# Two score levels and odd tokens' own scores in one matmul, even tokens' own scores by a sum over partitions

## The chip, the cores and the metric

The kernel runs on one core of one Trainium2 chip, as one launch. The metric is the device time of that core in microseconds (us). A core has TensorE for matmuls (PE in the profile, PEld for its weight loads), VectorE (DVE), ScalarE (ACT), GpSimd (POOL), and SyncE (SP), whose queue issues most of the transfers here. Each works through its own queue in order; semaphores tie the queues together. Matmul results land in PSUM, everything else lives in SBUF, both with 128 partitions.

## The reference

One step of a decoder layer: a gated feed-forward block, a mixer with two kinds of recurrences, and a second feed-forward block, for 256 tokens of a new sequence (the prompt) and 8 sequences of 4 new tokens each (the samples, 32 tokens). The change lies in the recurrences of the mixer:

```python
def gated_linear_scan(q, k, v, log_a, s0):
    """S_t = diag(exp(log_a_t)) S_{t-1} + k_t^T v_t ; o_t = q_t S_t."""
    ...
    def step(s, inp):
        qi, ki, vi, gi = inp
        cum = jnp.cumsum(gi, axis=2)
        diff = cum[:, :, :, None, :] - cum[:, :, None, :, :]
        decay = jnp.where(causal, jnp.exp(jnp.where(causal, diff, 0.0)), 0.0)
        scores = jnp.sum(qi[:, :, :, None, :] * ki[:, :, None, :, :] * decay, axis=-1)
        o = (jnp.einsum('bhts,bhsv->bhtv', scores, vi)
             + jnp.einsum('bhtd,bhdv->bhtv', qi * jnp.exp(cum), s))
```

The score of the tokens t and s (s not after t) is the sum over the 128 key dimensions d of q[t,d] k[s,d] times the product of the decay factors of the tokens s+1 to t. For s = t it is plainly q[t] k[t], the token's own score. There are 4 heads with 256 values (GLA) and 8 heads with 128 values (HGRN2).

## The kernel before, in words

All matrices with tokens are held transposed: feature on the partition, the 288 tokens (256 of the prompt, then 32 of the samples) along the row. A dense product is a loop over 16 tiles of the input (`block`, L455 on). Its weights come from HBM by SP's queue (L61, L63), are split into a high and a low part by ScalarE (L86, `wh`) and VectorE (L87, `wl`), and each product is three matmuls with 288 moving columns (L464 to L466). These are the large matmuls of this document. A block works on four PSUM tiles out of a pool of five (`mmp`), and its evacuation (`evac`) reads them at its end.

The mixer runs the blocks `qk0`, `v0`, `qk1`, `v1`, `hfq0`, `hi0`, `hfq1`, `hi1`, `hfq2`, `hfq3` and four `gate` blocks. The recurrences are six scans of two heads each (two for GLA, four for HGRN2). A scan is a Python generator. `block` calls `tick` after each of its 16 input tiles, that is after 12 large matmuls, and a tick runs the generator to its next `yield`, so that scan work is written between the large matmuls. A scheduler then sets the final order on each engine: it can move an instruction ahead of or behind others of its engine, as its data and buffers allow.

A scan finds the scores by doubling. At level `lv`, with h = 2^lv, the tokens lie in pairs of runs of h tokens: scores between a left run and the right run beside it are one level's share. `Q` is q times the decay since the start of its run, `k` is scaled by the decay to the end of its run; `update(lv)` (L803) multiplies the right halves of `Q` and the left halves of `k` by the factors that take them to the next level. Steps 0 to 8 of a scan:

- step 0: `own` (L790) multiplies k with q, 128 by 128 tokens, four matmuls (two heads, two halves of the prompt) into the PSUM tile `sc_d`; only the diagonal is wanted. VectorE forms Q = q * f (L873).
- step n, for n from 1 to 8: `score(n-1)` (L817) multiplies `k` (up to 128 weight columns) with the right-half columns of `Q` (64 moving columns), again four matmuls; at levels 0 and 1 also two small ones for the samples (L836), and at level 0 two for the samples' own scores (L840). Then the result of the step before goes to the score matrix `Dg` (prompt) and `Ds` (samples) by predicated copies under the masks `mk` (`own_put` L800, `put` L844: L855, L861, L865). Then `update(n-1)`: L811 for `Q`, L813 for `k`, L815 for the factors.

Level 7 is written to `X`, a part of the tile `rp` (L847). PSUM tiles of the scans come from a pool of three (`aux`), which transposes, output products and norms share. After step 8 come the transposes of the keys (`key_t`), the output products (`out`), the new states (`final`, `sample`) and the heads' norms (`norm_a` to `norm_c`). The samples' states are loaded by SP (L787) into four buffers `s0`, each of which comes free when POOL has stored the state before (L975); ScalarE and VectorE split a loaded state (L950, L951).

Two buffer names matter besides. `z` and `mx` are tags of a pool with two buffers each: `z` holds the scaled result of an `hfq` or `gate` evacuation, `mx` an intermediate of the `hfq` evacuation (L1125 to L1130) and of `norm_c` (L1014). The masks are loaded once as integers (`mi32`, L690) and cast to bytes by POOL (`mk`, L706).

Of the kernel before, what the change touches and what calls it, by code (L numbers as in the profile page):

```python
# [16 lines left out]
P = 128  # L17
# [98 lines left out]
def trunk_kernel(ctx, tc, x_prompt, x_sample, state_gla, state_hgrn, norm_gains, f1_in, f1_out, f2_in, f2_out,  # L116
# [540 lines left out]
    def mixer(pn, border):  # L657
        with ExitStack() as mx:
# [26 lines left out]
            def setup():  # L685
# [18 lines left out]
                G.memset(Dg, 0.0)  # L704
                G.memset(Ds, 0.0)
                G.tensor_copy(mk, mi32)  # L706
                for a in range(2):
# [56 lines left out]
            def scan(d, Vt, V32, Vs, gla, ytile0, s0, sp_out, ss_out):  # L764
# [24 lines left out]

                def own():  # L790
                    ps = auxtile("sc_d")
                    for i in range(2):
                        for a in range(2):
                            c = (i * 2 + a) * P
                            PE.matmul(ps[:, c:c + P], k[:, a, i * P:(i + 1) * P], q[:, a, i * P:(i + 1) * P],
                                      start=c == 0, stop=True, skip_group_check=True)
                    return ps

                def own_put(ps):
                    V.copy_predicated(Dflat, mk[:, 448:576].unsqueeze(1).broadcast_to([P, 4, P]),  # L800
                                      ps.rearrange("p (a c) -> p a c", c=P))

# [14 lines left out]
                def score(lv):  # L817
# [8 lines left out]
                    for i in range(2):  # L826
                        for a in range(2):
# [3 lines left out]
                                      start=c == 0, stop=True, skip_group_check=True)  # L831
                    if h <= 2:
                        for a in range(2):
                            c = 256 + a * 16
                            r = Q[:, a, TP:T].rearrange("p (n two k) -> p n two k", two=2, k=h)[:, :, 1, :]
                            PE.matmul(ps[0:TS, c:c + 16], k[:, a, TP:T], r, start=False, stop=True, skip_group_check=True)  # L836
                    if h == 1:
                        for a in range(2):
                            c = 288 + a * TS
                            PE.matmul(ps[0:TS, c:c + TS], k[:, a, TP:T], q[:, a, TP:T],  # L840
                                      start=False, stop=True, skip_group_check=True)
                    return ps

                def put(lv, ps):  # L844
# [4 lines left out]
                    if h == 64:  # L849
# [6 lines left out]
                                      ps[0:n, 0:256].rearrange("p (j n k) -> p j n k", j=4, k=h))  # L856
                    if h <= 2:
                        dst = Ds[0:TS].rearrange("p a (n two k) -> p (a n) two k", two=2, k=h)[:, :, 1, :]
                        n = 16 // h
                        for a in range(2):  # L860
                            V.copy_predicated(dst[:, a * n:(a + 1) * n, :],  # L861
                                              m[0:TS, 0:16].rearrange("p (n k) -> p n k", k=h),
                                              ps[0:TS, 256 + a * 16:272 + a * 16].rearrange("p (n k) -> p n k", k=h))
                    if h == 1:
                        V.copy_predicated(Ds[0:TS], mk[0:TS, 448:448 + TS].unsqueeze(1).broadcast_to([TS, 2, TS]),  # L865
                                          ps[0:TS, 288:352].rearrange("p (a c) -> p a c", c=TS))

                K3 = acc[:, 0:6 * TS].rearrange("p (a n t) -> p a n t", a=2, n=3)
                pss = {}
                for step in range(LEVELS + 1):  # L870
                    if step == 0:
                        pss[-1] = own()
                        V.tensor_tensor(Q, q, d["f"], op=ALU.mult)  # L873
                    else:
                        pss[step - 1] = score(step - 1)
                        if step == 1:
                            own_put(pss.pop(-1))
                        else:
                            put(step - 2, pss.pop(step - 2))
                        update(step - 1)  # L880
# [233 lines left out]
            def ev_hgrn(d, g):  # L1114
                def ev(f, ps):
                    z = tmp.tile([P, T], F32, name="z", tag="z")
                    ls = tmp.tile([P, T], F32, name="lsg", tag="lsg")
                    V.tensor_tensor(z, ps, rt, op=ALU.mult)
                    log_sigmoid(ls, z)
                    if f >= 2:  # L1120
                        act(ls, ls, AF.Exp)
                        V.scalar_tensor_tensor(d["q"][:, f - 2, :], z, QSCALE, ls, op0=ALU.mult, op1=ALU.mult)
# [4 lines left out]
                    V.tensor_tensor(m, ls, z, op=ALU.subtract)  # L1127
                    act(m, m, AF.Exp)
                    act(ls, ls, AF.Exp)
                    V.tensor_scalar(d["k"][:, f, :], m, omlb[:, hd:hd + 1], None, op0=ALU.mult)  # L1130
                    V.tensor_scalar(d["f"][:, f, :], ls, omlb[:, hd:hd + 1], lb[:, hd:hd + 1], op0=ALU.mult, op1=ALU.add)
# [144 lines left out]
```

## Time and profile before

| | |
|---|---|
| median of 3 runs | 2314.31 us (2312.02 to 2318.01) |
| profiled execution | 2314.71 us |
| its span | 2312.9 us |
| granted TensorE clock, mean | 0.997 |
| busy: TensorE, VectorE, ScalarE | 99%, 61%, 44% of the span |

The span is the time from the first to the last instruction of the profiled execution; its own time also counts what lies around them. Busy times count an engine while an instruction of it is in flight; matmuls overlap, so TensorE's cost of a matmul is read from the distance between starts and not from the duration shown. A line of a view names the engine, the line of the kernel, the operation and `out<-in` by the program's names. The chain of waits follows the work that ended last back to its releasers. The page itself and the other views are quoted in the prediction, where they are used.

### The profile page before, as it was taken

Reading aid. Unit: us, or ns where it says so; the run is one execution under the profiler, and the core shown is the slowest. Engines: PE = TensorE matmul, PEld = TensorE weight load, DVE = VectorE, ACT = ScalarE, POOL = GpSimd, SP = SyncE. Lnnn points to the kernel's source line nnn. Section 1 sums busy time; section 2 is a strip of 40 time slices with the busy share of each in tenths; the row PEclk is TensorE's granted clock in tenths of the full one; section 3 lists DMA queues with packets and bytes.
Section 4 is the critical chain, followed back from the end, with each engine's and each line's share of the span. In section 5 each row is a group of like instructions: output and inputs, shape, how many; then the busy total and the mean of one; then the engine's idle time right before and its main releaser. Section 6 shows DMA issues by size and latency. Waiting matters only on the chain.

```text
span 2312.9 us, 42140 instructions
## 1 busy us (share of the span) xinstructions
PE 2291.0 (99%) x17352; PEld 2276.1 (98%) x17352; DVE 1421.2 (61%) x2314; ACT 1012.7 (44%) x1555; POOL 64.4 (3%) x110
## 2 busy tenths in 40 slices
PE   9999999999999999999999999999999999999998
PEld 8999999999999999999999999999999999999998
DVE  7545545554556568787889854854555555545545
ACT  6443333333334446454555554544333333333345
POOL 0000000000000001001001100100000000000000
PEclk9999999999999999999999999999999999999999
DMA  7555555555555545555555555455555555555553
GB/s 214 164 166 164 165 166 168 168 165 164 167 167 186 157 151 159 152 152 171 149 169 156 159 184 167 129 160 172 165 165 167 169 164 163 165 164 166 165 164 115
DMA packets 217008, 378.16 MB, mean 163 GB/s; under 512 B 15362, under 2 KB 52400, under 8 KB 216816
## 3 DMA queue, kind: packets, MB, share of 16 engines
q1 hardware_dynamic: 211264, 365.48, 52.6%
q0 software_dynamic: 3376, 9.81, 1.3%
q8 instruction: 136, 2.23, 0.4%
q10 hardware_dynamic: 2176, 0.18, 0.1%
q14 instruction: 56, 0.46, 0.1%
HBM read 363.62 MB, written 11.80 MB: 162 GB/s over the span
## 4 chain that ended last, share of the span: by engine, by line
PE 94%; DVE 3%; issue 1%; DMA 1%; ACT 1%; POOL 0%; DVEq 0%; SPq 0%; POOLq 0%; ACTq 0%
PE gate L465 9%; PE gate L466 9%; PE gate L464 9%; PE out L465 8%; PE out L466 8%; PE out L464 8%; PE up L466 8%; PE up L464 8%; PE up L465 8%; PE hfq L464 2%; PE hfq L465 1%; PE mo L466 1%; PE mo L464 1%; PE mo L465 1%; PE hfq L466 1%; PE sc L830 1%
## 5 line engine op out<-in xcount | busy, mean ns | idle before, releaser
L87 DVE TENSOR_TENSOR wl<-raw,wh 128x1024 fp32r<-128x1024 f32 (+1 forms) x674 | 821.1, 1219 | 629.1 <-ACT wh L86 626.5
L86 ACT ACTIVATE wh<-raw 128x1024 fp32r<-128x1024 f32 (+1 forms) x674 | 711.3, 1056 | 1073.3 <-PE gate L465 323.9
L465 PE MATMUL gate<-xl,wh 128*128 128x288 f32 x1660 | 489.2, 295 | 0.2 <-DVE xl L243 0.2
L464 PE MATMUL gate<-xh,wh 128*128 128x288 f32 x1660 | 488.4, 296 | 0.7 <-DVE z L1174 0.5
L466 PE MATMUL gate<-xh,wl 128*128 128x288 f32 x1660 | 488.7, 295 | 0.2 <-DVE wl L87 0.2
L465 PE MATMUL out<-hl,wh 128*128 128x288 f32 x1408 | 415.8, 295 | 0.0
L464 PE MATMUL out<-hh,wh 128*128 128x288 f32 x1408 | 415.6, 295 | 0.0
L466 PE MATMUL up<-xh,wl 128*128 128x288 f32 x1408 | 415.0, 295 | 0.0
L466 PE MATMUL out<-hh,wl 128*128 128x288 f32 x1408 | 415.0, 295 | 0.0
L464 PE MATMUL up<-xh,wh 128*128 128x288 f32 x1408 | 414.6, 294 | 0.3 <-DVE g L523 0.3
L465 PE MATMUL up<-xl,wh 128*128 128x288 f32 x1408 | 414.8, 295 | 0.0
L465 PEld LDWEIGHTS gate<-xl,wh 128*128 128x128 f32 x1660 | 311.7, 188 | 1.1 <-DVE xl L243 1.0
L464 PEld LDWEIGHTS gate<-xh,wh 128*128 128x128 f32 x1660 | 310.5, 188 | 1.6 <-DVE z L1174 0.7
L466 PEld LDWEIGHTS gate<-xh,wl 128*128 128x128 f32 x1660 | 311.4, 188 | 0.7 <-DVE wl L87 0.7
L466 PEld LDWEIGHTS out<-hh,wl 128*128 128x128 f32 x1408 | 264.7, 188 | 0.0
L464 PEld LDWEIGHTS up<-xh,wh 128*128 128x128 f32 x1408 | 264.1, 188 | 0.6 <-DVE g L523 0.5
L464 PEld LDWEIGHTS out<-hh,wh 128*128 128x128 f32 x1408 | 264.6, 188 | 0.0
L465 PEld LDWEIGHTS out<-hl,wh 128*128 128x128 f32 x1408 | 264.5, 188 | 0.0
L466 PEld LDWEIGHTS up<-xh,wl 128*128 128x128 f32 x1408 | 264.2, 188 | 0.1
L465 PEld LDWEIGHTS up<-xl,wh 128*128 128x128 f32 x1408 | 264.2, 188 | 0.1
L583 DVE TENSOR_TENSOR y<-out,y 128x288 f32<-128x288 f32 x288 | 121.4, 452 | 104.5 <-PE out L466 101.7
L464 PE MATMUL hfq<-xh,wh 128*128 128x288 f32 x256 | 78.7, 307 | 0.0
(342 smaller groups left out, 2581.6 us busy)
## 6 DMA issues: line engine op xcount, KB each, us to landing
raw<-in_ffn_w_in_dram SPq DMA_DIRECT2D x352, 512.0 KB, 3.6
raw<-in_ffn_w_out_dram SPq DMA_DIRECT2D x176, 512.0 KB, 3.7
raw<-in_mix_w_in_dram SPq DMA_DIRECT2D x64, 512.0 KB, 3.7
raw<-in_mix_w_in_dram SPq DMA_DIRECT2D x96, 256.0 KB, 3.3
raw<-in_mix_w_out_dram SPq DMA_DIRECT2D x32, 512.0 KB, 3.8
out_dram<-s POOLq DMA_DIRECT2D x32, 256.0 KB, 3.3
s<-in_state_gla_dram SPq DMA_DIRECT2D x16, 256.0 KB, 3.6
s<-in_state_hgrn_dram SPq DMA_DIRECT2D x16, 256.0 KB, 3.4
```

Source lines behind the costliest of these rows:

```text
L86: i1 = self.nc.scalar.activation(h[:, c], raw[:, c], AF.Copy).ins
L87: i2 = self.nc.vector.tensor_tensor(l[:, c], raw[:, c], h[:, c].bitcast(F32), op=ALU.subtract).ins
L464: yield lambda: PE.matmul(dst, w[0][:, c:c + P], parts[0], start=start, stop=False)
L465: yield lambda: PE.matmul(dst, w[0][:, c:c + P], parts[1], start=False, stop=False)
L466: yield lambda: PE.matmul(dst, w[1][:, c:c + P], parts[0], start=False, stop=stop)
L583: V.tensor_tensor(y[k], ps, y[k], op=ALU.add)
L830: PE.matmul(ps[0:m, c:c + 64], k[:, a, i * P:i * P + m], r, start=c == 0, stop=True, skip_group_check=True)
```

## The change

Levels 0 and 1 and the own scores of odd tokens are computed by one group of four matmuls, and the own scores of even tokens by an elementwise product that a matmul with a matrix of equal entries sums over the partitions.

After `update(0)`, `k` of odd tokens is still the plain k, and `k` of even tokens carries the factor of the token behind it. So the product of this `k` with the plain q of odd tokens holds both: at s = t the own score of the odd token, at s = t - 1 its level-0 score. The same `k` with the right halves of `Q` after `update(0)` is level 1. A new tile `R` holds the two sets of 64 columns side by side, `R[:, a, 0]` the plain q of odd tokens and `R[:, a, 1]` the right halves of `Q` for level 1, copied by ScalarE (`lay`). The level-0 mask gets the diagonal of the odd tokens added. `rp` holds, before it is needed for `X`, the product of q and k of the even tokens, 144 columns for each head.

```diff
@@ setup @@
                 G.memset(Ds, 0.0)
+                V.tensor_tensor(mi32[:, 0:64], mi32[:, 0:64],
+                                mi32[:, 448:576].rearrange("p (n two) -> p n two", two=2)[:, :, 1], op=ALU.max)
                 G.tensor_copy(mk, mi32)
@@ scan @@
-                def own():
-                    ps = auxtile("sc_d")
+                R = sp[0].tile([P, 2, 2, T // 2], F32, name="R", tag="R", bufs=1)
+                own = rp.rearrange("p (a c) -> p a c", a=2)
+                def lay(lv, src):
+                    h = 1 << lv
+                    S.activation(R[:, :, lv, :].rearrange("p a (n k) -> p a n k", k=h), halves(src, h, True), AF.Copy)
+                def score01():
+                    ps, po = auxtile("sc01"), auxtile("sc_o")
                     for i in range(2):
                         for a in range(2):
                             c = (i * 2 + a) * P
-                            PE.matmul(ps[:, c:c + P], k[:, a, i * P:(i + 1) * P], q[:, a, i * P:(i + 1) * P],
+                            PE.matmul(ps[:, c:c + P], k[:, a, i * P:(i + 1) * P], R[:, a, :, i * 64:(i + 1) * 64],
                                       start=c == 0, stop=True, skip_group_check=True)
-                    return ps
-                def own_put(ps):
-                    V.copy_predicated(Dflat, mk[:, 448:576].unsqueeze(1).broadcast_to([P, 4, P]),
-                                      ps.rearrange("p (a c) -> p a c", c=P))
+                    PE.matmul(po[:, 0:T], onesD, rp, start=True, stop=True, skip_group_check=True)
+                    for a in range(2):
+                        c = T + a * TS
+                        PE.matmul(po[0:TS, c:c + TS], k[:, a, TP:T], R[:, a, :, P:P + TS // 2],
+                                  start=False, stop=True, skip_group_check=True)
+                    return ps, po
+                def put01(ps, po):
+                    ...
+                    for i in range(2):
+                        V.copy_predicated(v[:, i, :, :, 0], eye(P, 64).unsqueeze(1).broadcast_to([P, 2, 64]),
+                                          ov[:, :, i * 64:(i + 1) * 64])
+                    V.copy_predicated(sv[:, :, :, 0], eye(TS, 16).unsqueeze(1).broadcast_to([TS, 2, 16]),
+                                      ov[0:TS, :, P:])
+                    for lv in range(2):
+                        ...
+                        V.copy_predicated(dst, m.rearrange("p (n k) -> p n k", k=h).unsqueeze(1).broadcast_to(dst.shape),
+                                          ps.rearrange("p (j l n k) -> p j l n k", j=4, l=2, k=h)[:, :, lv])
+                        dst = Ds[0:TS].rearrange("p a (n two k) -> p a n two k", two=2, k=h)[:, :, :, 1, :]
+                        for a in range(2):
+                            c = T + a * TS + lv * 16
+                            V.copy_predicated(dst[:, a], m[0:TS, 0:16].rearrange("p (n k) -> p n k", k=h),
+                                              po[0:TS, c:c + 16].rearrange("p (n k) -> p n k", k=h))
@@ score and put: the sample parts of levels 0 and 1 (L832 to L841, L857 to L866) go @@
@@ the steps @@
                     if step == 0:
-                        pss[-1] = own()
+                        V.scalar_tensor_tensor(own.unsqueeze(3), halves(q, 1, False), float(D), halves(k, 1, False),
+                                               op0=ALU.mult, op1=ALU.mult)
                         V.tensor_tensor(Q, q, d["f"], op=ALU.mult)
+                        lay(0, q)
+                    elif step == 1:
+                        update(0)
+                        lay(1, Q)
                     else:
-                        pss[step - 1] = score(step - 1)
-                        if step == 1:
-                            own_put(pss.pop(-1))
-                        else:
+                        pss[step - 1] = score01() if step == 2 else score(step - 1)
+                        if step == 3:
+                            put01(*pss.pop(1))
+                        elif step > 3:
                             put(step - 2, pss.pop(step - 2))
                         update(step - 1)
@@ norm_c @@
-                    m = tmp.tile([P, T], F32, name="hm", tag="mx")
+                    m = tmp.tile([P, T], F32, name="hm", tag="z")
@@ ev_hgrn @@
-                    m = tmp.tile([P, T], F32, name="mx", tag="mx")
-                    V.tensor_tensor(m, ls, z, op=ALU.subtract)
-                    act(m, m, AF.Exp)
+                    V.tensor_tensor(z, ls, z, op=ALU.subtract)
+                    act(z, z, AF.Exp)
                     act(ls, ls, AF.Exp)
-                    V.tensor_scalar(d["k"][:, f, :], m, omlb[:, hd:hd + 1], None, op0=ALU.mult)
+                    V.tensor_scalar(d["k"][:, f, :], z, omlb[:, hd:hd + 1], None, op0=ALU.mult)
```

In the changed kernel the four matmuls of `score01` with the prompt stand in line 809, the one with the matrix `onesD` of entries 1/2048 in line 811 (hence the factor `D` in the product), and the two for the samples in line 814. Per scan, 18 matmuls in three groups (4; 4 + 2 + 2; 4 + 2) become 7 in one group at step 2. The copies of that group stand in step 3, behind `score(2)`. The tag `mx` is gone, which makes room for `R`.

More of the change, by code (lines that the diff above doesn't have):

```diff
@@ L831, in score @@
                                       start=c == 0, stop=True, skip_group_check=True)
[L832 to L841, printed above, removed]
                     return ps
@@ L856, in put @@
                                       ps[0:n, 0:256].rearrange("p (j n k) -> p j n k", j=4, k=h))
[L857 to L866, printed above, removed]
                 K3 = acc[:, 0:6 * TS].rearrange("p (a n t) -> p a n t", a=2, n=3)
```

8 lines of the change are left out of this document (added).

## The prediction

> **What bounds the kernel now.** I read the page first: its busy times, then its chain of waits.
>
> ```profile
> span 2312.9 us, 42140 instructions
> ...
> PE 2291.0 (99%) x17352; PEld 2276.1 (98%) x17352; DVE 1421.2 (61%) x2314; ACT 1012.7 (44%) x1555; POOL 64.4 (3%) x110
> ...
> PE 94%; DVE 3%; issue 1%; DMA 1%; ACT 1%; POOL 0%; DVEq 0%; SPq 0%; POOLq 0%; ACTq 0%
> ```
>
> TensorE is busy for all but 22 us of the span, and 94% of the chain that ended last runs on it. An instruction taken off TensorE therefore shortens the kernel by the time for which it holds up the next one, as long as no new wait opens; what moves to VectorE (61%) or ScalarE (44%) costs nothing as long as it comes in time. The scans run between 925 and 1330 us, where VectorE is fuller than its average. So two questions decide: how much TensorE time goes, and whether VectorE still delivers in the scan stretches. For the second I read who waits for whom.
>
> ```profile
> PE tp_v L728 <- DVE vt L745: 3.3, 1, 3.3
> ...
> ACT hl L950 <- DMA s<-in_state_hgrn_dram: 5.9, 2, 3.0
> ```
>
> The columns are us in total, times, longest. The only long wait of TensorE inside the mixer is this one of 3.3 us. It hangs on a state load: ScalarE stands 3.0 us at a state tile that has not landed, the split of the next weights behind it is late, and VectorE's queue with the V tile behind that. Everything else on TensorE in the scans is work.
>
> **What the removed matmuls cost.** A matmul's own duration (some 290 ns) overlaps with its neighbours', so I take starts: from the start of the last large matmul before a group to the start of the second large one behind it, less the two large ones. This is the timeline of TensorE in the first scan (start, us, engine, line, what); an fp32 matmul shows as two records, so x8 is four matmuls.
>
> ```profile
> 927.38 0.29 PE L465 MATMUL qk<-xl,wh 128*128 128x288 f32 x1
> 927.51 0.29 PE L466 MATMUL qk<-xh,wl 128*128 128x288 f32 x1
> 927.64 1.05 PE L795 MATMUL sc_d<-q_g,k_g 128*128 128x128 f32 x8
> 928.45 0.38 PE L464 MATMUL qk<-xh,wh 128*128 128x288 f32 x1
> 928.66 0.29 PE L465 MATMUL qk<-xl,wh 128*128 128x288 f32 x1
> ...
> 929.98 0.29 PE L466 MATMUL qk<-xh,wl 128*128 128x288 f32 x1
> 930.11 0.99 PE L830 MATMUL sc<-Q,k_g 128*127 128x64 f32 x8
> 931.03 0.30 PE L836 MATMUL sc<-Q,k_g 128*32 128x16 f32 x4
> 931.18 0.29 PE L840 MATMUL sc<-q_g,k_g 128*32 128x32 f32 x4
> 931.40 0.40 PE L464 MATMUL qk<-xh,wh 128*128 128x288 f32 x1
> 931.64 0.29 PE L465 MATMUL qk<-xl,wh 128*128 128x288 f32 x1
> ...
> 932.97 0.29 PE L466 MATMUL qk<-xh,wl 128*128 128x288 f32 x1
> 933.10 0.99 PE L830 MATMUL sc<-Q,k_g 128*126 128x64 f32 x8
> 934.01 0.30 PE L836 MATMUL sc<-Q,k_g 128*32 128x16 f32 x4
> 934.24 0.40 PE L464 MATMUL qk<-xh,wh 128*128 128x288 f32 x1
> 934.48 0.30 PE L465 MATMUL qk<-xl,wh 128*128 128x288 f32 x1
> ```
>
> Large matmuls follow each other at 0.13 us (927.38 to 927.51). Own scores: 928.66 - 927.51 - 0.26 = 0.89 us. Level 0 with its sample matmuls: 931.64 - 929.98 - 0.26 = 1.40 us. Level 1: 934.48 - 932.97 - 0.26 = 1.25 us. Together 3.54 us per scan, all of it removed. The reader should see two things. Four matmuls with 64 moving columns take as long as four with 128 (0.92 us from 930.11 to 931.03, 0.81 us from 927.64 to 928.45), because each loads its 127 or 128 weight columns anew; and every group pays for its entry and exit, the first large matmul behind it needing some 0.2 us instead of 0.13.
>
> **What the new matmuls cost.** The four of L809 have the shape of the own-score matmuls, 128 weight columns and 128 moving ones: 0.89 us with one entry and exit. The sum over partitions is an fp32 matmul with 128 weight columns and 288 moving ones; `zp` has that shape:
>
> ```profile
> 957.47 0.29 PE L465 MATMUL v<-xl,wh 128*128 128x288 f32 x1
> 957.60 0.65 PE L1108 MATMUL zp<-y,y 128*128 128x288 f32 x2
> 957.87 0.51 PE L466 MATMUL v<-xh,wl 128*128 128x288 f32 x1
> 958.21 0.30 PE L464 MATMUL v<-xh,wh 128*128 128x288 f32 x1
> ```
>
> 958.21 - 957.47 - 0.26 = 0.48 us. The two sample matmuls (32 weight columns, 32 moving) have L840 as their row: 0.15 us at the least, the distance from L836 to L840 in level 0 (931.03 to 931.18), when a group of the same width stands before them. At the most it is what level 1 pays above four plain matmuls, 1.25 - 0.89 = 0.36 us; there the change from 128 to 32 columns is included. The new ones too stand behind wide ones, so I take 0.36. New sum 0.89 + 0.48 + 0.36 = 1.73 us, saving 1.81 us per scan; with 0.15 it is 2.02. Six scans: 10.9 us, at most 12.1.
>
> **What is added elsewhere.** VectorE loses the copy of the own scores and one small sample copy per scan; it gains the product of even tokens and three copies for them. The rows, from the views of the tiles `sc_d`, `sc` and `z` (ns minimum, median, maximum):
>
> ```profile
> L800 DVE COPY_PREDICATED Dg<-mk,sc_d x6: 719/738/746, 929.1 to 1247.3; 128x512 f32<-128x512 uint8 x6
> ```
>
> ```profile
> L855 DVE COPY_PREDICATED Dg<-mk,sc x36: 417/435/737, 933.2 to 1272.3; 127x256 f32<-127x256 uint8 x6, 126x256 f32<-126x256 uint8 x6, 124x256 f32<-124x256 uint8 x6, 120x256 f32<-120x256 uint8 x6
> ...
> L861 DVE COPY_PREDICATED Ds<-mk,sc x24: 168/218/240, 933.8 to 1259.4; 32x16 f32<-32x16 uint8 x24
> ```
>
> ```profile
> L759 ACT ACTIVATE ls<-z x28: 427/440/447, 920.6 to 1295.5; 128x288 f32<-128x288 f32 x28
> ...
> L1122 DVE SCALAR_TENSOR_TENSOR q_h<-z,lsg x8: 448/450/459, 1037.3 to 1227.1; 128x288 f32<-128x288 f32 x8
> ```
>
> Out: 0.74 (L800) and 0.2. In: 0.45 for the product (as L1122), two copies of half the size of L800, 0.37 each, and one small of 0.2. That is +0.5 us per scan on VectorE; ScalarE gets two copies into `R` of 0.44 us (as L759). Here is the scan with the least room, and the stretch of the long wait (columns: stretch, length, then busy us and instructions of PE, PEld, DVE, ACT, POOL, then the granted clock):
>
> ```profile
> 1123.00:1152.00 29.00, 29.00 (x241) 28.56 (x240) 25.89 (x65) 11.29 (x21) 0.75 (x1) 1.00 0.48 142
> ```
>
> ```profile
> 1067.00:1071.00 4.00, 0.73 (x6) 0.49 (x4) 1.43 (x3) 1.67 (x3) 0.00 (x0) 0.91 0.45 149
> 1071.00:1074.00 3.00, 2.98 (x14) 2.96 (x15) 2.70 (x8) 2.21 (x7) 0.00 (x0) 0.50 0.72 216
> 1074.00:1077.00 3.00, 3.00 (x14) 2.97 (x14) 1.61 (x6) 1.58 (x7) 0.00 (x0) 0.50 0.61 152
> ```
>
> VectorE is busy for 25.89 of 29.00 us there. Less 1.8 us of TensorE and plus 0.5 us of VectorE, it is 26.4 of 27.2: it still fits, but thinly. So the additions cost nothing in sum, and something at places. In the built program's order the level-2 scores stand 12 large matmuls behind the joint group in the first three scans, but only 7 and 6 behind it in the fourth and fifth (0.9 and 0.8 us). In that time VectorE must update `k`, 0.45 us. If VectorE is free that holds; if a weight split (1.22 us, below) is in front, TensorE waits most of it. I charge half a split, 0.6 us, at each of the two, and 0.3 us at the start of `gate0`, where the key transposes of the fifth scan now stand three matmuls behind its last score. Give-back 1.5 us, between 0 and some 4 (three full splits).
>
> **The shared buffers.** `mx` is gone and its values live in `z`, of which there are two. The third evacuation of an `hfq` block therefore waits for the first `k_h` and no longer for `mx`:
>
> ```profile
> 1032.12 0.46 DVE L1127 TENSOR_TENSOR mx<-lsg,z 128x288 f32<-128x288 f32 x1
> 1032.68 0.46 DVE L1118 TENSOR_TENSOR z<-hfq,rt 128x288 f32<-128x288 f32 x1
> 1033.06 1.22 DVE L87 TENSOR_TENSOR wl<-raw,wh 128x1024 fp32r<-128x1024 f32 x1
> 1034.19 0.36 DVE L1130 TENSOR_SCALAR k_h<-mx,omlb 128x288 f32<-128x288 f32 x1
> ```
>
> Its PSUM tile is released up to 2 us later (1032.12 to 1034.19), at four block ends. The next block's fourth tile needs that buffer, and TensorE's queue stops there if it is late; in the built order this tile stands three matmuls further back behind the first `hfq` block. Bounds 0 and 4 x 2 = 8 us; I take nothing, since the reordering covers most of it, and keep the rest for the range. The new operation on the mask, on VectorE, waits for a load issued some 50 us earlier. The cast of the mask behind it on POOL now follows 909 us, and the first copy that uses it comes after 930: nothing. ScalarE's and SP's order around the 3.3 us wait is as before, so that wait stays.
>
> **Sum.** The profiled execution took 2314.71 us: the span of 2312.9 and 1.8 outside. 2314.7 - 10.9 + 1.5 = 2305.3. It stands 0.4 us above the median of the runs, 2314.31; so 2305.0 for the median, 0.4% less.
>
> **Rivals.** (1) The long wait goes, because the whole scan is timed otherwise. It costs 3.3 us of idling and then 6 us at clock 0.50 (1071 to 1077), half of which, 3.0 us, is lost: 6.3 us, giving 2298.7. Against it: every instruction that leads to it keeps its order.
>
> (2) The wait stays, but the slow clock behind it does not come: 2302.0. For it: the three runs already lie 6 us apart with one program. [...]
>
> (3) A second wait like it, or the later PSUM releases at half their bound: 4 to 6.3 us given back, 2309 to 2311.5. For it: two state loads of the fifth and sixth scans change places with weight loads in SP's queue. Against it: ScalarE's waits for such states are two in all (the row above), both at the place of the 3.3 us wait.
>
> (4) Slower: VectorE becomes the bound at step 3. Nine copies stand together where before they lay in three steps: 2 x 0.72, 2 x 0.37, 0.2 and 4 x 0.2, some 3.2 us. With the updates (3 x 0.43) and one split that is 5.7 us, against two steps of 12 large matmuls and a score, 2 x (1.57 + 0.89) = 4.9. Level 3 needs both the update and a PSUM tile that these copies free (three tiles, and the joint group holds two). It decides once TensorE waits over 1.8 us per scan, so with two splits in between; 3 us per scan give 2314.7 - 10.9 + 18 = 2321.8. Against it: in the built order `k` is updated ahead of most of these copies.
>
> (5) The change removes nothing, since the new group costs as much: excluded, 1.73 against 3.54 by rows of the same shapes.
>
> **Chances.** A run tells 0.3% (6.9 us, so below 2307.4) from no change. My forecast, 2302.5 to 2307.4: 0.56. Rival 1: 0.08; rival 2: 0.06; both faster, so 0.70. Rival 3: 0.20, within. Rival 4: 0.10, slower. The range of 2298.5 to 2312 leaves out rival 4 and the ends of 1 and 3.
>
> **What would show it.** Right: the joint group takes 1.5 to 1.75 us between large matmuls, TensorE has 66 matmuls fewer (132 records), its busy time falls by about 11 us, and the 3.3 us wait with its slow clock is still there. Wrong in size: level-2 or level-3 scores, `hi` or `gate` matmuls appear among TensorE's waits on VectorE with more than 3 us in total. Wrong in kind: the joint group near 3 us, or the mixer's stretch no shorter.

## The result, and the profile after

| kernel | median | runs | ratio to before |
|---|---|---|---|
| before | 2314.48 us | 2312.02 to 2318.01 (6) | |
| after | 2304.18 us | 2301.99 to 2305.13 (6) | 0.9956, 95% 0.9946 to 0.9966 |

The change saves 10.3 us. The profiled execution of the changed kernel took 2303.51 us. Its page, busy times and the chain of waits:

```profile
span 2301.7 us, 41887 instructions
...
PE 2279.4 (99%) x17220; PEld 2262.0 (98%) x17220; DVE 1424.5 (62%) x2327; ACT 1017.9 (44%) x1567; POOL 65.1 (3%) x110
...
PE 93%; DVE 3%; ACT 2%; DMA 1%; issue 1%; POOL 0%; SPq 0%; DVEq 0%; ACTq 0%; POOLq 0%
```

TensorE has 132 records fewer (17352 to 17220) and 11.6 us less of busy time; VectorE has 3.3 us more, ScalarE 5.2. TensorE still carries the chain. The joint group of the first scan in the timeline of TensorE (start, us, engine, line, what):

```profile
931.47 0.29 PE L465 MATMUL qk<-xl,wh 128*128 128x288 f32 x1
931.60 0.30 PE L466 MATMUL qk<-xh,wl 128*128 128x288 f32 x1
931.74 1.05 PE L809 MATMUL sc<-R,k_g 128*128 128x128 f32 x8
932.63 0.65 PE L811 MATMUL sc_o<-rp,onesD 128*128 128x288 f32 x2
933.21 0.31 PE L814 MATMUL sc_o<-R,k_g 128*32 128x32 f32 x4
933.45 0.40 PE L464 MATMUL qk<-xh,wh 128*128 128x288 f32 x1
933.69 0.30 PE L465 MATMUL qk<-xl,wh 128*128 128x288 f32 x1
```

By the prediction's measure it takes 933.69 - 931.60 - 0.26 = 1.83 us in place of 3.54: 1.71 us less per scan, 10.3 us for six. (The second, third and sixth scan have 1.82 us too; the fourth has 2.42, with the wait for `R` below, and the fifth 1.91.) The whole fall of 10.3 us would then be explained with nothing given back, but TensorE's waits say otherwise (us in total, times, longest; after):

```profile
PE gate L464 <- DVE z L1197: 1.1, 2, 0.6
PE tp_v L731 <- DVE vt L748: 1.1, 1, 1.1
...
PE a_lr L1125 <- DVE ahl L703: 0.8, 1, 0.8
...
PE sc L809 <- ACT R L801: 0.3, 1, 0.3
```

Of before, beside the lines that the prediction shows:

```profile
PE sc L830 <- DVE k_h L813: 0.7, 1, 0.7
...
PE gate L464 <- DVE z L1174: 0.5, 1, 0.5
```

Several things happened at once. New small waits opened: for `ahl`, for `z` at the `gate` blocks, for `R`. A small one went, the 0.7 us for `k_h` at the level-2 scores of the sixth scan; the prediction had counted everything but the long wait as work. And the 3.3 us wait for the V tile in the third scan, which the prediction kept, was 1.1 us, with the clock at 1.00 behind it. Whether that last gain is the change's or the run's was the main question for the experiments.

**Where the small waits come from.** The first lies at the start of the mixer. Timeline of before (the square bracket is the idle time before an instruction and what ended it):

```profile
909.97 2.35 DVE L87 TENSOR_TENSOR wl<-raw,wh 128x1024 fp32r<-128x1024 f32 x2
...
912.24 0.41 DVE L703 TENSOR_TENSOR ahl<-araw,ahl 128x256 fp32r<-128x256 f32 x1
...
912.71 0.40 PE L1101 MATMUL a_lr<-xh,ahl 128*128 128x288 f32 x1 [0.16 <-DVE ahl L703]
```

And of after:

```profile
909.85 0.22 DVE L707 TENSOR_TENSOR mi<-mi 128x64 int32<-128x64 int32 x1
...
910.13 0.83 POOL L709 CAST mk<-mi 128x576 uint8<-128x576 int32 x1 [23.13 <-DVE mi L707]
910.36 2.86 DVE L87 TENSOR_TENSOR wl<-raw,wh 128x1024 fp32r<-128x1024 f32 x2
910.91 1.09 POOL L711 MEMSET qm<- 128x576 f32 x2
...
913.14 0.41 DVE L703 TENSOR_TENSOR ahl<-araw,ahl 128x256 fp32r<-128x256 f32 x1
...
913.61 0.40 PE L1125 MATMUL a_lr<-xh,ahl 128*128 128x288 f32 x1 [0.79 <-DVE ahl L703]
```

The operation on the mask (L707) sits on VectorE where TensorE is waiting for VectorE, and POOL's cast waits 23 us for it, so that the cast and the clears behind it run beside two weight splits, which now take 2.86 us in place of 2.35. TensorE's wait is 0.6 us longer.

The second is the copy into `R` in the fourth scan. Timeline of ScalarE and TensorE of after:

```profile
1123.20 1.06 ACT L86 ACTIVATE wh<-raw 128x1024 fp32r<-128x1024 f32 x1 [2.71 <-DMA raw<-in_mix_w_in_dram]
1124.16 0.45 ACT L801 ACTIVATE R<-Q 128x288 f32<-128x288 f32 x1
...
1124.66 1.16 PE L809 MATMUL sc<-R,k_h 128*128 128x128 f32 x8 [0.34 <-ACT R L801]
```

ScalarE's queue stood at a weight tile that had not landed, its cast came first, and the copy into `R` behind it was late. The old scores read `Q` directly and did not wait for ScalarE at all.

### The profile page after: what moved, and what is told of

Same layout as the page of the kernel before. It is cut to its first block, busy times and chain, and to the rows that moved or that the text cites. A ratio compares the mean times of both kernels' runs of the same rounds, so it can differ in the third digit from the quotient of the medians.

```text
span 2301.7 us, 41887 instructions
## 1 busy us (share of the span) xinstructions
PE 2279.4 (99%) x17220; PEld 2262.0 (98%) x17220; DVE 1424.5 (62%) x2327; ACT 1017.9 (44%) x1567; POOL 65.1 (3%) x110
## 4 chain that ended last, share of the span: by engine, by line
PE 93%; DVE 3%; ACT 2%; DMA 1%; issue 1%; POOL 0%; SPq 0%; DVEq 0%; ACTq 0%; POOLq 0%
PE gate L464 9%; PE gate L466 9%; PE gate L465 9%; PE out L465 8%; PE out L466 8%; PE out L464 8%; PE up L466 8%; PE up L464 8%; PE up L465 8%; PE mo L466 1%; PE mo L464 1%; PE mo L465 1%; PE hfq L464 1%; PE hfq L466 1%; PE hfq L465 1%
## 5 line engine op out<-in xcount | busy, mean ns | idle before, releaser
L464 PE MATMUL gate<-xh,wh 128*128 128x288 f32 x1660 | 488.8, 296 | 1.5 <-DVE z L1197 1.1
L466 PE MATMUL gate<-xh,wl 128*128 128x288 f32 x1660 | 489.1, 295 | 0.2 <-DVE wl L87 0.2
L464 PE MATMUL out<-hh,wh 128*128 128x288 f32 x1408 | 415.6, 295 | 0.0
L466 PE MATMUL up<-xh,wl 128*128 128x288 f32 x1408 | 415.0, 295 | 0.0
L466 PE MATMUL out<-hh,wl 128*128 128x288 f32 x1408 | 415.0, 295 | 0.0
L464 PE MATMUL up<-xh,wh 128*128 128x288 f32 x1408 | 414.6, 294 | 0.3 <-DVE g L523 0.3
L464 PEld LDWEIGHTS gate<-xh,wh 128*128 128x128 f32 x1660 | 310.6, 188 | 3.2 <-DVE z L1197 1.6
L466 PEld LDWEIGHTS gate<-xh,wl 128*128 128x128 f32 x1660 | 311.6, 188 | 0.5 <-DVE wl L87 0.4
L466 PEld LDWEIGHTS out<-hh,wl 128*128 128x128 f32 x1408 | 264.7, 188 | 0.0
L464 PEld LDWEIGHTS up<-xh,wh 128*128 128x128 f32 x1408 | 264.1, 188 | 0.6 <-DVE g L523 0.5
L464 PEld LDWEIGHTS out<-hh,wh 128*128 128x128 f32 x1408 | 264.6, 188 | 0.0
L466 PEld LDWEIGHTS up<-xh,wl 128*128 128x128 f32 x1408 | 264.2, 188 | 0.1
L464 PE MATMUL hfq<-xh,wh 128*128 128x288 f32 x256 | 77.7, 304 | 0.0
```

The lines of the kernel that those rows point to most:

```text
L464: yield lambda: PE.matmul(dst, w[0][:, c:c + P], parts[0], start=start, stop=False)
L466: yield lambda: PE.matmul(dst, w[1][:, c:c + P], parts[0], start=False, stop=stop)
```

## The experiments

The wait and the slow clock are told first, since they decide how much of the fall belongs to the change. Each group of kernels has its own runs of the kernel before, and ratios are to those.

| kernel | median | runs | ratio to before, 95% |
|---|---|---|---|
| z_only | 2314.05 us | 2311.78 to 2316.24 (11) | 1.0004, 0.9995 to 1.0013 |
| share_only | 2306.29 us | 2304.29 to 2308.40 (6) | 0.9971, 0.9960 to 0.9983 |
| after_timed | 2301.91 us | 2301.31 to 2303.12 (5) | 0.9953, 0.9940 to 0.9965 |
| ones_twice | 2306.05 us | 2305.18 to 2307.75 (6) | 0.9971, 0.9959 to 0.9982 |
| copies_twice | 2305.53 us | 2303.76 to 2307.55 (6) | 0.9966, 0.9953 to 0.9978 |
| five_states | 2299.81 us | 2298.34 to 2300.98 (5) | 0.9943, 0.9930 to 0.9955 |
| before_five | 2308.75 us | 2308.40 to 2309.12 (8) | 0.9974, 0.9963 to 0.9984 |
| five_mask | 2300.66 us | 2300.02 to 2301.53 (5) | 0.9939, 0.9925 to 0.9952 |
| lays_twice | 2302.99 us | 2301.78 to 2304.84 (5) | 0.9949, 0.9937 to 0.9962 |

The medians of before in the three groups (first two rows, next four, last three) were 2312.93, 2313.30 and 2314.67 us. after_timed is the changed kernel without an edit, timed beside the three rows below it. Expected for it were 8.5 to 9.5 us less than before (ratio 0.9960) if the long wait is an accident of the run, or 6.8 us (0.9971) if the first ratio held a share of luck; 0.9960 lies inside its interval and 0.9971 outside.

Some readings below compare two profiles by their large matmuls (L464 to L466). Every kernel here has the same 16152 of them in nearly the same order, so that the starts of the two profiles can be subtracted one by one, and the difference shows where in the mixer time is lost or won.

**Both kernels, profiled again (before_again, after_again).** No edit.

> The kernel before, profiled a second time. Open is whether the 3.3 us wait of TensorE for the V tile in the third scan (tp_v) and the stretch at clock 0.50 behind it belong to the program or to the one profiled execution. If they belong to the program: the wait is 3.0 to 3.6 us again, the clock is 0.50 for some 6 to 7 us behind it, and the mean granted clock is 0.997. If they belong to the execution (the second hgrn state load took 5.9 us to land there): the wait is anything from 1 to 3.3 us, and with under 2.5 us there is no slow clock; the span is then 4 to 6 us shorter, near 2308, and the time of such a run lies at the lower end of what the kernel shows (2312).

> The changed kernel, profiled a second time. If the wait and the slow clock belong to the program: the tp_v wait is 0.8 to 1.4 us again, clock 1.0 throughout the scans, span 2301 to 2303. If they belong to the execution, either can be seen here: a wait up to 3.3 us, and then 0.50 for some 6 us and a span of 2305 to 2308. The joint group takes 1.8 us in the first scan in either case.

The wait was 2.0 us in before, with the clock at 1.00 behind it, and 3.0 us in the changed kernel, with 3.4 us at 0.50 (spans 2309.4 and 2304.1 us). So neither kernel has it at a fixed size. The expected 2.5 us, under which there was to be no slow clock, were the author's guess and did not hold either: the table below has the clock at 0.50 behind 2.3 and 2.2 us. This is the chain behind it in after_again, from the timeline of all engines:

```profile
1060.54 0.97 SPq L790 DMA_DIRECT2D s<-in_state_hgrn_dram  x2
...
1066.53 0.42 ACT L974 ACTIVATE hl<-s 128x256 fp32r<-128x256 f32 x1 [1.43 <-DMA s<-in_state_hgrn_dram]
1066.86 1.04 ACT L86 ACTIVATE wh<-raw 128x1024 fp32r<-128x1024 f32 x1
...
1067.93 1.22 DVE L87 TENSOR_TENSOR wl<-raw,wh 128x1024 fp32r<-128x1024 f32 x1 [3.24 <-ACT wh L86]
1069.07 0.25 DVE L748 TENSOR_TENSOR vt<-hi,rt 128x96 f32<-128x96 f32 x1
...
1069.38 0.32 PE L731 MATMUL tp_v<-ident,vt 128*96 128x128 f32 x1 [2.97 <-DVE vt L748]
```

The second state is issued about 1061.1 and lands at 1066.45; 2.93 us later (one cast, one split, one piece of the V tile) TensorE goes on. That time is 2.92 to 2.94 us in all nine profiles with four state buffers in which this load ends the wait. What differs is how long the transfer takes and how long after its issue TensorE arrives at the wait; the wait is the transfer plus 2.93 us less that time (all from the records of the transfer and of TensorE; the slow stretch from windows of 1 us):

| profile | transfer, us | issue to TensorE's arrival, us | wait, us | at clock 0.50, us |
|---|---|---|---|---|
| before | 5.90 | 5.5 | 3.3 | 6.8 |
| before_again | 4.25 | 5.2 | 2.0 | 0 |
| z_only | 4.35 | 5.0 | 2.3 | 3.4 |
| share_only | 4.49 | 5.3 | 2.2 | 6.8 |
| after | 3.96 | 5.8 | 1.1 | 0 |
| after_again | 5.31 | 5.3 | 3.0 | 3.4 |
| after_timed | 3.70 | 5.8 | 0.8 | 0 |
| ones_twice | 3.87 | 5.7 | 1.1 | 0 |
| copies_twice | 3.79 | 5.8 | 0.9 | 0 |

Four profiles without the sum over partitions average a wait of 2.5 us, five with it 1.4. The one long wait among the five shows that it can still come, and so few draws do not show that the change shortens it. In the tenth profile with four buffers, lays_twice, the instructions stand in another order and TensorE waits 0.2 us there.

**A fifth buffer for the states (five_states, before_five).** The load waits for a buffer that POOL must store first (SP's queue stands at L787 for stores of states 22 times in before, 74.8 us in all, and at L790 22 times in after, 68.5 us). The same edit in both kernels:

```diff
-   t = sp[0].tile([P, nb, dv], F32, name="s0", tag="s0", bufs=4)
+   t = sp[0].tile([P, nb, dv], F32, name="s0", tag="s0", bufs=5)
...
-   kd = sp[0].tile([P, 2, P], F32, name="kd", tag="kd")
+   kd = sp[0].tile([P, 2, P], F32, name="kd", tag="kd", bufs=1)
```

> The changed kernel with five buffers for the samples' states in place of four (and one buffer for kd in place of two, for the room). Theory: the second state of the third scan is late because its load waits for a buffer, so that ScalarE stands behind it, VectorE's weight split behind ScalarE, and TensorE behind that; with a fifth buffer the load goes out 2 to 4 us earlier, the wait for the V tile is under 1 us, the clock stays 1.0, and the median falls by 1 to 4 us below the changed kernel. Rival: the load waits for its place in SP's queue and for the transfers around it and lands as late as before: no change, the wait is 1 to 3 us.

> The kernel before with five buffers for the states (and one for kd), as five_states is the changed kernel with them. In nine profiles the next matmul after the long wait starts 2.93 us after the second state has landed, so an earlier load takes the wait and its slow clock away here too, and the two kernels with five buffers can be compared without that accident. Theory (the change itself is worth some 7.5 us, and the rest of the 10 to 11 us between the medians is that the long wait and its slow clock were shorter and rarer in the changed kernel): this kernel takes 2307 to 2308, 7 to 8 us above five_states, and 5 to 6 us below the kernel before. Rival (the change itself is worth all of it): 2310 to 2311, 10 to 11 us above five_states and only 2 to 3 below the kernel before.

The timeline of five_states at the same place:

```profile
1057.20 0.97 SPq L790 DMA_DIRECT2D s<-in_state_hgrn_dram  x2
...
1060.26 0.42 ACT L974 ACTIVATE hl<-s 128x256 fp32r<-128x256 f32 x1 [2.67 <-DMA s<-in_state_hgrn_dram]
...
1063.85 0.44 PE L730 MATMUL tp_v<-ident,vt 128*128 128x128 f32 x2 [0.64 <-DVE vt L747]
```

The wait is 0.6 us, and the clock stays at 1.00, in either kernel. The way there was not quite the expected one. Counted from the same large matmul, the load of this state goes out only 0.4 to 1.2 us earlier and not 2 to 4; but it is now the first of a pair of loads and no longer the second. In the nine profiles of the table the first of the two took 2.7 to 3.5 us from issue to landing, and the second, issued 0.6 to 1.5 us behind it, 3.7 to 5.9. With five buffers the state that TensorE depends on took 3.0 us (five_states) and 3.1 (before_five).

The fifth buffer saves the kernel before 5.9 us (2314.67 to 2308.75), and the spread of its runs shrinks from 5.1 us to 0.7: most of what its runs differed by are waits for states. The changed kernel gains only 2.1 us by it (2301.91 to 2299.81), and its spread stays (1.8 and 2.6 us). These savings are not the long wait's alone. By the large matmuls, the fifth buffer saves time at two places. One is the long wait with its slow clock: 4.6 and 1.3 us in the two profiles of before, 0.4, 3.2 and 0.2 in after, after_again and after_timed. The other lies at the end of the first scan and the start of the second (975 to 1000 us), where ScalarE stands at the states of the GLA heads: 1.5 and 1.2 us in before, but 2.9, 2.7 and 2.4 us in the changed kernel. ScalarE's waits for those states in after:

```profile
ACT hl L974 <- DMA s<-in_state_gla_dram: 12.4, 5, 4.6
```

And in five_states:

```profile
ACT hl L974 <- DMA s<-in_state_gla_dram: 1.7, 1, 1.7
```

So with four buffers the change makes the waits for the GLA states some 1.3 us dearer, which neither the prediction nor the expectations saw.

Between the two kernels with five buffers there is 0.9974 - 0.9943 = 0.0031, or 7.2 us, which two such ratios give to some 4 us either way; the spans differ by 8.9 us, and by the large matmuls the mixer is 8.8 us shorter. five_mask below, which has five buffers too and ran beside before_five, is 8.1 us below it (2308.75 - 2300.66), and its slowest run is 6.9 us below the fastest of before_five. The first line of the page of before_five:

```profile
span 2306.7 us, 42135 instructions
```

And of five_states:

```profile
span 2297.8 us, 41880 instructions
```

So without these waits the change is worth 7 to 9 us, and the rest of the 10 to 11 us between the medians is that the waits for states were cheaper in the changed kernel, by 5.9 - 2.1 = 3.8 us in balance: the GLA states dearer by 1.3 us, the long wait cheaper by some 5 us. That split is an estimate from the medians and five profiles. The rival's 2310 to 2311 us for before_five lies within its interval (0.9963 to 0.9984 of 2314.67 is 2306.1 to 2311.0), though its eight runs end at 2309.12. What the rival says of differences falls: 2 to 3 us below the kernel before, where the interval has 3.7 to 8.6, and 10 to 11 us above the changed kernel with five buffers, where the pairs have 7.2 to 8.9.

**The shared buffers alone (z_only).** The kernel before with the edits of `mx` to `z` and nothing else:

```diff
-   m = tmp.tile([P, T], F32, name="hm", tag="mx")
+   m = tmp.tile([P, T], F32, name="hm", tag="z")
...
-   V.tensor_tensor(m, ls, z, op=ALU.subtract)
-   act(m, m, AF.Exp)
+   V.tensor_tensor(z, ls, z, op=ALU.subtract)
+   act(z, z, AF.Exp)
...
```

> The kernel before with only the buffers shared: mx is gone and its values live in z. The prediction took nothing for it: within 1.5 us of the kernel before, 2314.4, TensorE busy 2291 us. Rival: the later releases cost up to 8 us, 2316 to 2322, with waits of TensorE for the evacuations of the blocks hfq at four block ends. A second rival: this part alone moves the long wait of the third scan (its order on VectorE around the state weights changes), and the time falls by 3 to 6 us, to 2308 to 2311, with no clock of 0.50 behind it.

1.0004, so between -1.2 and +3.0 us. The prediction's zero stands; 8 us more is excluded, and so are the 3 to 6 us less of the second rival.

**The shared operand alone (share_only).** The sum over partitions is undone; even tokens' own scores are matmuls at step 0:

```diff
-   V.scalar_tensor_tensor(own.unsqueeze(3), halves(q, 1, False), float(D), halves(k, 1, False),
-                          op0=ALU.mult, op1=ALU.mult)
+   pss[-1] = own()
...
+   PE.matmul(ps[:, c:c + 64], k[:, a, i * P:(i + 1) * P],
+             q[:, a, i * P:(i + 1) * P].rearrange("p (n two) -> p n two", two=2)[:, :, 0],
+             start=c == 0, stop=True, skip_group_check=True)
...
-   PE.matmul(po[:, 0:T], onesD, rp, start=True, stop=True, skip_group_check=True)
```

The first `PE.matmul` stands in `own`, four times, with two for the samples behind it, and VectorE copies the result at step 1.

> The changed kernel with the sum over partitions undone: even tokens' own scores are six small matmuls at the first step of a scan (four of 128 x 64 moving columns, two for the samples), as one level is; levels 0, 1 and the odd tokens' own scores still share their operand. Theory (a group costs TensorE what its stretch between large matmuls shows): it adds 1.25 us (a group of that form in the profile before) and takes away 0.58 us (the sum's step in the changed kernel), +0.67 us per scan, +4.0 us in all: 2308.2, ratio to before 0.9973. Rival (VectorE's and ScalarE's new work gives back half of the gain in small waits): the product of 0.45 us and two copies leave VectorE here, so waits go and the time is 2304 to 2306. Rival (the gain is mostly the long wait of the third scan, moved by the new order): 2302 to 2305 if that wait stays short, 2310 to 2314 if it is back.

0.9971 against 0.9953 for after_timed is 4.2 us; the theory said 4.0. But the closeness is in part luck, since these medians hold the waits for states as well. By the large matmuls share_only is 6.8 us longer in the mixer than after_timed; 4.4 us of that is the third scan, where its wait was 2.2 us with 6.8 us of slow clock. The other five scans make 2.4 us, where the theory has 5 x 0.67 = 3.4. So the sum over partitions is worth 2.4 to 4 us, and the larger part of the gain is the shared operand's. Of the rivals, the second gave 2302 to 2305 or 2310 to 2314, and neither came. The first (2304 to 2306, with small waits gone) is not excluded: the interval is 2303.7 to 2309.0.

**The sum twice (ones_twice).** L811 is written a second time behind itself:

```diff
    PE.matmul(po[:, 0:T], onesD, rp, start=True, stop=True, skip_group_check=True)
+   PE.matmul(po[:, 0:T], onesD, rp, start=True, stop=True, skip_group_check=True)
```

> The changed kernel with the sum over partitions issued a second time in each scan, into the same tile. Theory (what a small group costs is TensorE's time, step by step): +0.48 to 0.58 us per scan, +2.9 to 3.5 us over the changed kernel. Rival (the product and the copies behind it on VectorE set the pace, TensorE waits there anyway): under 1 us more.

4.1 us more than after_timed (2306.05 - 2301.91). The fastest of its runs is 2.1 us above the slowest of after_timed, so the rival's 1 us falls: TensorE's time is what counts. The profile shows the step itself: the joint group takes 2.30 or 2.31 us in place of 1.82 or 1.83 in the four scans without a wait, 0.48 us more, and 3.1 us more in the six together, as the theory has it. The rest is in waits, the longest of them 1.0 us of a later level's scores (L870) for VectorE.

**The copies twice (copies_twice).**

```diff
+   put01(*pss[1])
    put01(*pss.pop(1))
```

> The changed kernel with the nine predicated copies of the joint group written twice: VectorE gets 3.4 us more per scan (2 x 0.72, 2 x 0.45, 0.25, 4 x 0.2), 20 us in all, all of it at step 3. Theory (VectorE has room, since k is updated ahead of most copies and TensorE's next score does not need them): 0 to 4 us more than the changed kernel. Rival (VectorE is the bound at step 3, as the prediction's fourth case had it): most of the 3.4 us shows in each scan, 12 to 20 us more, with waits of TensorE for level 3 and for the evacuations.

3.6 us more (2305.53 - 2301.91), at the upper end of the theory and far from the rival's 12. The page has VectorE with 54 instructions more and 12.1 us more of busy time than after_timed (1436.6 and 1424.3 us):

```profile
PE 2279.6 (99%) x17220; PEld 2262.0 (98%) x17220; DVE 1436.6 (62%) x2381; ACT 1017.4 (44%) x1567; POOL 63.4 (3%) x110
```

The expectation had 20 us, from durations that overlap (in after the copy L828 starts at 934.47 and lasts 0.25 us, and the next copy starts at 934.54). Less than a third of the added time reaches the end: VectorE has room at step 3, though not enough to take another 2 us per scan free.

**ScalarE's copies twice (lays_twice).**

```diff
    lay(0, q)
+   lay(0, q)
...
    lay(1, Q)
+   lay(1, Q)
```

> The changed kernel with both of ScalarE's copies into R written twice: 0.9 us more of ScalarE per scan, 5.3 us in all. TensorE waited 0.3 to 0.4 us for R at one joint group in each profile of the changed kernel. Theory (the joint group of most scans has R in time): 0 to 1.5 us more than the changed kernel, with waits for R of up to 1 us in total. Rival (the copies into R set the start of the joint group): 0.4 to 0.9 us in each scan, 2.5 to 5.3 us more.

1.1 us more than after_timed by the medians, but 0.9 us less by the ratios (0.9949 against 0.9953, another group), so in the time it can't be told from nothing, and the rival's 2.5 to 5.3 us are not there. The waits for `R`, 0.2 us in after_timed, show where the copies count:

```profile
PE sc L809 <- ACT R L801: 0.9, 2, 0.5
```

Two joint groups wait for `R` in place of one. `R` is in time at the other four, so it is a cost of a place and not of every scan.

**The mask on POOL (five_mask).** five_states with the operation on the mask moved:

```diff
-   V.tensor_tensor(mi32[:, 0:64], ..., op=ALU.max)
+   G.tensor_tensor(mi32[:, 0:64], ..., op=ALU.add)
```

> The changed kernel with five state buffers and with the operation on the mask on POOL in place of VectorE (a sum in place of a maximum, the same for these masks). In the changed kernel VectorE does it at 909.9 us, between the first products of the mixer, and the cast on POOL follows at once beside two weight splits of VectorE that take 2.86 us in place of 2.35; the split of ahl is 0.9 us later and TensorE waits 0.8 us for it in place of 0.2. Theory: the wait for ahl is 0.2 us again, and the time falls by 0.6 us below five_states, 2299.2. Rival (the wait moves to the next instruction in VectorE's queue): no change.

The place is mended (timeline of five_mask):

```profile
910.53 2.35 DVE L87 TENSOR_TENSOR wl<-raw,wh 128x1024 fp32r<-128x1024 f32 x2
...
912.80 0.42 DVE L703 TENSOR_TENSOR ahl<-araw,ahl 128x256 fp32r<-128x256 f32 x1
...
913.27 0.40 PE L1125 MATMUL a_lr<-xh,ahl 128*128 128x288 f32 x1
```

The splits take 2.35 us again and `a_lr` does not wait. But in this profile the wait behind the states is longer again, 1.4 us in place of 0.6 in five_states, since the load it hangs on landed 0.8 us later, counted from the same large matmul:

```profile
PE tp_v L730 <- DVE vt L747: 1.4, 1, 1.4
```

In the time the mask can't be told: 0.9939 and 0.9943 are the same within their intervals, and the medians of the two groups (2300.66 and 2299.81 us) stand in the other order, with before 1.4 us higher as well. Both are 13 to 14 us below the kernel before, and all runs of five_states lie below all of after_timed, which ran beside it.

The changed kernel with an own buffer for `mx` was not tried; there was no room in SBUF.

## Why the prediction was right

The time, 2304.2 us against 2305.0, was right, and so was its main reason: a group's price is what it adds between the large matmuls. Of its signs of being right, TensorE's 132 records and its 11.6 us of busy time came; the joint group took 1.83 us and not 1.5 to 1.75, and the 3.3 us wait with its slow clock was not there. Point by point:

- **Removed and new matmuls.** Predicted 3.54 - 1.73 = 1.81 us per scan, measured 1.71. The term that was off is the sum over partitions: 0.58 us from its start to the next group's (932.63 to 933.21) in place of 0.48. Behind it stand the narrow weights of L814 and not a large matmul; their load began at 933.21, 0.38 us after the load before it had ended. Six scans: 10.3 us in place of 10.9. ones_twice bears the pricing out: the second sum, which has no narrow weights of its own behind it, adds 0.48 us. share_only does so less sharply, with 2.4 us by the trace and 4.2 by the medians for 4.0.
- **Give-back.** Predicted 1.5 us. Without the waits for states, 10.3 us of groups leave 7.2 (ratios) to 8.9 us (spans): 1.4 to 3.1 us given back. The size was fair, the places were wrong. By the large matmuls of before_five and five_states, 0.6 us goes at the mask and 0.6 at the joint group of the fourth scan, which waits for `R`. The 0.6 us at the level-2 scores of the fourth and fifth scan did not come: in the fourth, L869 starts at once behind the large matmuls (1127.38 to 1127.52):

```profile
1127.38 0.30 PE L464 MATMUL hi<-xh,wh 128*128 128x288 f32 x1
1127.52 0.98 PE L869 MATMUL sc<-Q,k_h 128*124 128x64 f32 x8
1128.30 0.38 PE L465 MATMUL hi<-xl,wh 128*128 128x288 f32 x1
```

- **The mask, taken as nothing.** It cost TensorE 0.6 us. The prediction looked at who reads the mask (after 930 us) and not at who stands behind the operation in VectorE's queue, nor at POOL's work that it pushes beside VectorE's splits.
- **`R`, taken as ScalarE time with no price.** It cost 0.2 to 0.7 us at one joint group in each profile of the changed kernel, with four buffers or five, since TensorE now waits for a queue that it did not wait for before.
- **"That wait stays."** This was the step that failed. The order of the instructions that lead to the long wait did not change, as the prediction said, but the wait's size does not follow from order: it is the transfer's time plus 2.93 us less the time until TensorE arrives. Its range within one program (2.0 and 3.3 us before, 0.8 to 3.0 after) shows what one profile could not: the 3.3 us and the slow clock on which the prediction's own time rested were one draw. That the waits for states are cheaper after the change, by 3.8 us in balance, came unforeseen. TensorE arrives a little later there (5.3 to 5.8 us after the issue against 5.0 to 5.5 without the sum over partitions); why the transfers took 3.7 to 5.3 us and 4.3 to 5.9 without it stays open. The prediction also looked at the waits for the HGRN2 states alone, two in all; ScalarE waits for the GLA states too, and there the change lost some 1.3 us.
- **The sum.** -10.9 + 1.5 = -9.4 us was predicted. Measured is -10.3 to -11.4, made of 7 to 9 us for the change itself and some 2 to 4 us of the waits for states. That the forecast is so close is partly luck: an optimistic group time and a missed gain cancel.
- **Rivals.** The first (the wait goes) came in part. The second (the wait without the slow clock) was seen in before_again, so it was open within the kernel before already. The fourth (VectorE the bound at step 3) is refuted by copies_twice. The third, shared buffers, is refuted by z_only; no second long wait appeared. The fifth, that the new group costs as much as the old ones, falls by 1.83 against 3.54 us.

## What to carry to other kernels

Price a small matmul group by the starts of the large ones around it, and price what stands next to it too: the sum took 0.58 us in front of narrow weights, and the same shape 0.48 in front of a large matmul. Before a wait enters a sum, profile the kernel twice: the wait behind a transfer was a draw here (2.0 and 3.3 us before, 0.8 to 3.0 after), and its median price could be read by giving the loads a buffer more in both kernels, once the other waits that the buffer took away were looked at too. An operation that runs once is not free because its result is needed late (the mask cost TensorE 0.6 us); look at the queue in which it stands.

## What the runs showed of the hardware

**The clock stood at 0.50 for 3.4 or 6.8 us, behind waits of 2.2 us and more.** Windows of after_again (stretch, length, busy us and instructions of PE, PEld, DVE, ACT, POOL, then the granted clock):

```profile
1066.00:1070.00 4.00, 1.03 (x9) 0.80 (x8) 2.07 (x5) 1.94 (x4) 0.00 (x0) 1.00 0.44 150
1071.00:1074.00 3.00, 3.00 (x15) 2.98 (x14) 2.79 (x8) 2.54 (x11) 0.00 (x0) 0.50 0.84 244
```

Windows of share_only:

```profile
1065.00:1068.00 3.00, 0.85 (x7) 0.61 (x5) 1.44 (x3) 1.67 (x3) 0.00 (x0) 0.96 0.76 244
1068.00:1071.00 3.00, 3.00 (x14) 2.97 (x15) 2.71 (x8) 2.21 (x7) 0.00 (x0) 0.50 0.55 168
1071.00:1074.00 3.00, 3.00 (x15) 2.97 (x15) 1.60 (x6) 1.58 (x7) 0.00 (x0) 0.50 0.79 205
```

Windows of before_again:

```profile
1066.00:1070.00 4.00, 2.02 (x17) 1.79 (x16) 2.15 (x6) 2.02 (x5) 0.00 (x0) 1.00 0.73 230
1070.00:1074.00 4.00, 4.00 (x36) 4.00 (x34) 3.73 (x11) 4.00 (x17) 0.48 (x1) 1.00 0.75 208
```

With a wait of 2.2 us (share_only) the clock fell while TensorE was still idle, and stood at 0.50 for 6.8 us; with 3.0 us (after_again) it fell 1.6 us after work had begun again, for 3.4 us; with 2.0 us (before_again) it did not fall. At this place the slow stretch was 0, 3.4 or 6.8 us in all profiles. What decides between these was not shown.

**POOL beside VectorE.** Two splits with two operands in SBUF took 2.35 us in before and in five_mask, where POOL has no instruction from 900 to 920 us, and 2.86 us, 0.5 us more, in after with POOL's cast and clears beside them; whether the cast or the clears did it was not tried.
